# Modulation rows handed out along the mixer, and weight splits taken off GpSimd, in a hybrid DeltaNet layer

## The chip, the cores and the metric

The kernel runs on one core of a Trainium2 chip. The metric is the device time of one execution in microseconds (us). A core has TensorE (PE: matmuls, with weight loads shown as PEld), VectorE (DVE), ScalarE (ACT), GpSimd (POOL) and SyncE (SP), whose queue issues the transfers between memory and the on-chip buffers. Each engine takes its own instructions in the order in which they stand in its queue; semaphores hold one engine for another.

## What is computed

One decoder layer over 2048 tokens of width 1024. The vector c gives, through the weights w_ada, six rows of 1024 modulation values: shift, scale and gate for the mixer and for the feed-forward part.

```python
mod = (c_act @ w_ada[l] + b_ada[l])[:, None, :]
sh_m, sc_m, g_m, sh_f, sc_f, g_f = jnp.split(mod, 6, axis=-1)
h = rmsnorm(x, pre_mix_norm_w[l]) * (1.0 + sc_m) + sh_m
y = token_mixer(h, ...)
x = x + g_m * rmsnorm(y, post_mix_norm_w[l])
h = rmsnorm(x, pre_ffn_norm_w[l]) * (1.0 + sc_f) + sh_f
y = jnp.square(jax.nn.relu(h @ w_ff1[l])) @ w_ff2[l]
x = x + g_f * rmsnorm(y, post_ffn_norm_w[l])
```

The mixer projects h with w_in. One part is a gated delta rule with four heads (q, k, v through a short convolution, a recurrence over chunks whose state is carried from chunk to chunk, and an output gate z); the other is a gated short convolution of four groups (three projections each). Both go through w_out.

## The kernel before

The 2048 tokens are worked on in four blocks of 512, one behind the other; the change touches block 0, and three instructions at the start of block 1. A block is: norm and transpose of x, the mixer, the product with w_out (mix_out, L821), and the feed-forward part. Activations lie with the channels on the partitions. All projections are done with operands split in two parts (a rounded high part and the rest, "lo"), in three products: one tile of 128 output columns takes 8 x 3 = 24 matmuls of 128x512 (L336). The weights of a tile come as 512 KB from memory into a staging buffer (name w1s, 3 of them), are rounded by ScalarE (L250) and subtracted from (L251) by VectorE, or by GpSimd where the call says so, into a tile of the name w1h (3 of them). The first block keeps copies in memory for the later blocks (L288).

What the mixer does, by lines:

- L571 to L611: for two pairs of heads, twelve projections, each with a convolution (conv_silu, L430: ScalarE L436, VectorE three times L438, ScalarE L440), transposes (to_tm, L574) and sums of squares; pair_tail (L536) then forms for each pair the matrices Um and At, 16 of each of 128x128. Its last VectorE operation is L568.
- L622 to L649: the diagonal 32x32 blocks of Um go out to memory and come back side by side (L624, L630); VectorE inverts them by a substitution of 30 steps (L638, L640); the result goes out and comes back in place (L642 to L648).
- L657: block_inverse(t) builds block diagonals on GpSimd (L665) and does the rest of the inverse with short TensorE passes (L670 first). L695: scan(t) is one step of the recurrence over 128 tokens; its first products (L704) need only the state. block_inverse(t + 1) is written ahead of scan(t).
- L756 to L784: four projections for z, each evicted by one Silu on ScalarE (L762) into tiles of the name sb, then norm and gate of the recurrence's output. L786 to L812: the four short-conv groups, three projections each.
- L813: the gate and the second modulation are finished with column sums (L172, L192).

The modulation: w_ada has six parts of 1024 columns. Parts 0 and 1 are done at the start, part 5 in the feed-forward part. Here parts 2 (the mixer's gate, into the tile gate_m), 4 and 3 (scale and shift of the feed-forward part, into gate_f and a tile sb) are formed, each with eight rows of 128x1024, 24 in all. A row is one 512 KB load into a tile of the name w2h (3 of them, L129) and one VectorE operation on 128x1024 (L131 or L133). They were written as three jobs ahead of the first three short-conv groups (L618, L788).

What sets the order of the instructions: the program is written as quoted, and a scheduler lays each engine's queue out ahead of time, by data and buffers and in the order of the program where these leave a choice. So the place of an instruction in its queue is not the place of its line in the program. The projections for z and for the short-conv groups need nothing but h and weights, and the scheduler has put many of them ahead of the inverse. A tile of a name is given out in program order, and the next user of a buffer waits for the last reader of it. The accumulators of the projections (name acc) are four. Numbers behind a name (acc_1936) are running numbers of the tile in one kernel; they differ between the kernels.

Of the kernel before, what the change touches and what calls it, by code (L numbers as in the profile page):

```python
# [8 lines left out]
F32 = mybir.dt.float32  # L9
# [4 lines left out]
ALU = mybir.AluOpType  # L14

P = 128
# [4 lines left out]
TB = 512  # L21
# [11 lines left out]
def hybrid_layer(  # L33
# [90 lines left out]

    def ada_acc(part, acc):

        for k in range(KT):
            st = stage_w2h()
            nc.sync.dma_start(out=st, in_=w_ada[k * P:(k + 1) * P, part * DM:(part + 1) * DM])  # L129
            if k == 0:  # L130
                V.tensor_scalar(out=acc, in0=st, scalar1=c_act[:, 0:1], scalar2=None, op0=ALU.mult)  # L131
            else:
                V.scalar_tensor_tensor(out=acc, in0=st, scalar=c_act[:, k:k + 1], in1=acc,  # L133
                                       op0=ALU.mult, op1=ALU.add)
        return [acc[:, 0:TB], acc[:, TB:DM]]
# [294 lines left out]
    def conv_silu(ps, ft, dst):  # L430
# [6 lines left out]
        for w in range(3):  # L437
            V.scalar_tensor_tensor(out=tmp, in0=cb[:, w:w + TB], scalar=conv_w[:, w, ft:ft + 1],  # L438
                                   in1=tmp, op0=ALU.mult, op1=ALU.add)
        A.activation(out=dst, in_=tmp, func=AF.Silu)  # L440
# [82 lines left out]
    def mixer(b, hT, gates):  # L523
# [9 lines left out]
        rd = dram.tile([2, 4, 16, 32, 32], F32, name="rd")  # L533

        tails = []
        def pair_tail(pr, ssq, vfm):  # L536
# [12 lines left out]
            for hh in range(2):  # L549
# [7 lines left out]
                for tp0 in range(0, NT, 2):  # L557
# [4 lines left out]
                    for t in (tp0, tp0 + 1):  # L562
# [4 lines left out]
                                               op1=ALU.mult)  # L567
                        V.tensor_tensor(out=At[m // 8][:, m % 8, :], in0=pk[:, t - tp0, P:2 * P],  # L568
                                        in1=dt, op=ALU.mult)

        for pr in range(2):  # L571
# [17 lines left out]
            for hh in range(2):  # L589
                h = 2 * pr + hh  # L590
                for n, base in ((0, 4), (1, 0), (2, 8)):
                    if (pr, hh, n) == (0, 1, 1):
                        beta, eg, neg, dts = gates()
                    if early:
                        ps = early.pop(0)
                    else:
                        w = load_w1(w_in, (base + h) * P, (G, V, G)[n])
                        ps = ps_acc()
                        proj(ps, w, hT)
                    if n == 2:  # L600
                        vf = t2()
                        vfm.append(vf)
                    conv_silu(ps, base + h, vf if n == 2 else kq[h][:, n, :])
                    if tails and (hh, n) == (0, 1):
                        pair_tail(*tails.pop())
# [6 lines left out]

        if b == 0:
            gate_m = const.tile([P, DM], F32, name="gate_m")
            gate_f = const.tile([P, DM], F32, name="gate_f")
            ada["gate_m"], ada["gate_f"] = gate_m, gate_f
            acc_f = []
            jobs = [lambda: ada_acc(2, gate_m), lambda: acc_f.append(ada_acc(4, gate_f)),  # L618
                    lambda: acc_f.append(ada_acc(3, slot_b()))]

# [74 lines left out]
        def scan(t):  # L695
# [31 lines left out]
            for h0, m, um in pairs(t):  # L727
# [9 lines left out]
                for j in range(2):  # L737
                    h = h0 + j
                    V.scalar_tensor_tensor(out=S[h], in0=S[h], scalar=eg[:, 2, m + j:m + j + 1],
                                           in1=pg[:, j, P:2 * P], op0=ALU.mult, op1=ALU.add)  # L740
                V.tensor_tensor(out=om, in0=om, in1=pg[:, :, 0:P], op=ALU.add)

        wst = []
        block_inverse(0)
        for t in range(NT):
            if t + 1 < NT:
                block_inverse(t + 1)
            if t == NT - 1:
                for k in korder:
                    st = slot_a()  # L750
                    nc.sync.dma_start(out=st, in_=w_out[k * P:(k + 1) * P, :])
                    wst.append(st)
            scan(t)


        zs = [slot_b() for _ in range(2)]  # L756
        zh = [zs[h // 2][:, (h % 2) * TB:(h % 2 + 1) * TB] for h in range(NH)]
        for h in range(NH):
            w = load_w1(w_in, OFF_Z + h * P, (G, G, V, V)[h])
            ps = ps_acc()  # L760
            proj(ps, w, hT)
            A.activation(out=zh[h], in_=ps, func=AF.Silu)  # L762
# [23 lines left out]
        for f in range(4):  # L786
            if b == 0 and jobs:
                jobs.pop(0)()  # L788
            w = load_w1(w_in, OFF_SC + f * P)
# [23 lines left out]
        if b == 0:  # L813
            ada_gate(gate_m, 2, post_mix_norm_w)
            ada["f"] = [ada_affine(acc_f[0][i], acc_f[1][i], 100 + 4 * i, 68 + 4 * i, 92 + 4 * i, f"f{i}")
                        for i in range(2)]
# [348 lines left out]
```

## Time and profile before

| what | value |
| --- | --- |
| median of 3 runs | 2497.76 us (2494.24 to 2498.12) |
| the profiled execution | 2501.52 us, span 2499.8 us |
| TensorE busy | 2416.5 us (97%), 11874 matmuls |
| VectorE busy | 1764.7 us (71%) |
| ScalarE busy | 1170.9 us (47%) |
| GpSimd busy | 237.0 us (9%) |

The profiled execution is one run under the hardware profiler; its times are those of the rows below. A row of stretches gives the window, its length, and then for PE, PEld, DVE, ACT and POOL the busy time and in brackets the number of instructions, the granted TensorE clock as a share of full speed, the share of the transfer engines' time in use, and GB/s. A row by line gives line, engine, operation, out<-in and their shapes, count, busy time, mean duration, and behind the second bar how long the engine was idle just before these instructions and what ended that. Matmuls overlap, so the duration of one (0.39 us) is longer than the distance from one to the next.

### The profile page before, as it was taken

Reading aid. Unit: us, or ns where it says so; the run is one execution under the profiler, and the core shown is the slowest. Engines: PE = TensorE matmul, PEld = TensorE weight load, DVE = VectorE, ACT = ScalarE, POOL = GpSimd, SP = SyncE. Lnnn points to the kernel's source line nnn. Section 1 sums busy time; section 2 is a strip of 40 time slices with the busy share of each in tenths; the row PEclk is TensorE's granted clock in tenths of the full one; section 3 lists DMA queues with packets and bytes.
Section 4 is the critical chain, followed back from the end, with each engine's and each line's share of the span. In section 5 each row is a group of like instructions: output and inputs, shape, how many; then the busy total and the mean of one; then the engine's idle time right before and its main releaser. Section 6 shows DMA issues by size and latency. Waiting matters only on the chain.

```text
span 2499.8 us, 33806 instructions
## 1 busy us (share of the span) xinstructions
PE 2416.5 (97%) x11874; PEld 2011.4 (80%) x11874; DVE 1764.7 (71%) x3833; ACT 1170.9 (47%) x2402; POOL 237.0 (9%) x391
## 2 busy tenths in 40 slices
PE   5889999999999999999999999999999999999998
PEld 3678887788778888888878888888887888888887
DVE  6777795877885568576697657756679556857675
ACT  5533552444563245544466145544456424654432
POOL 2513010000040201000012020000002120100000
PEclk9999999999999999999999999999999999999999
DMA  7788489855664542544475544345557454344453
GB/s 246 266 292 267 168 292 310 283 177 169 202 234 156 172 153 103 156 147 127 136 245 193 184 154 143 102 135 152 160 164 249 143 169 168 110 144 135 125 161 101
DMA packets 297268, 449.53 MB, mean 180 GB/s; under 512 B 39189, under 2 KB 195978, under 8 KB 282250
## 3 DMA queue, kind: packets, MB, share of 16 engines
q1 hardware_dynamic: 295584, 447.27, 54.5%
q8 instruction: 94, 1.54, 0.3%
q14 instruction: 76, 0.62, 0.1%
q10 hardware_dynamic: 1514, 0.09, 0.0%
HBM read 376.01 MB, written 71.30 MB: 179 GB/s over the span
## 4 chain that ended last, share of the span: by engine, by line
PE 75%; DVE 13%; DMA 7%; ACT 3%; issue 2%; POOL 0%; SPq 0%; ACTq 0%; DVEq 0%
PE acc L336 41%; PE acc L341 24%; DVE t L438 2%; DMA w2h<-in_w_ff_dram 2%; DMA w2h<-in_w_ada_dram 1%; PE pd L704 1%; DMA w1s<-in_w_ff_dram 1%; PE pd L336 1%; DMA ws<-w2h 1%; DVE w1h L251 1%; DVE sb L935 1%; PE pd L560 1%; PE tp L265 1%; PE tp L692 1%; DVE sb L850 1%
## 5 line engine op out<-in xcount | busy, mean ns | idle before, releaser
L336 PE MATMUL acc<-h,w1h 128*128 128x512 f32 x5184 | 1219.6, 392 | 0.0
L336 PEld LDWEIGHTS acc<-h,w1h 128*128 128x128 f32 x5184 | 968.2, 188 | 196.0 <-ACT w1h L250 0.2
L341 PE MATMUL acc<-w1h,sa 128*128 128x512 f32 x2556 | 594.6, 392 | 7.9 <-ACT w1h L250 4.1
L341 PEld LDWEIGHTS acc<-w1h,sa 128*128 128x128 f32 x2556 | 478.3, 188 | 110.0 <-DVE w1h L251 7.0
L251 DVE TENSOR_TENSOR w1h<-w1s,w1h 128x1024 fp32r<-128x1024 f32 x333 | 406.5, 1221 | 152.8 <-ACT w1h L250 152.6
L250 ACT CAST w1h<-w1s 128x1024 fp32r<-128x1024 f32 (+1 forms) x343 | 359.6, 1048 | 289.2 <-PE acc L341 195.9
L959 DVE TENSOR_TENSOR t<-t 128x512 f32<-128x512 f32 (+1 forms) x148 | 91.3, 620 | 182.0 <-ACT t L958 179.2
L958 ACT ACTIVATE t<-acc 128x512 f32<-128x512 f32 (+1 forms) x132 | 73.7, 558 | 246.7 <-PE acc L336 246.3
L276 POOL TENSOR_TENSOR h<-t,h 128x256 fp32r<-128x256 f32 x70 | 59.6, 857 | 1251.9 <-ACT h L275 1246.6
L438 DVE SCALAR_TENSOR_TENSOR t<-cb,cols,t 128x512 f32<-128x512 f32 x144 | 119.1, 831 | 65.7 <-ACT t L436 63.9
L251 DVE TENSOR_TENSOR w2h<-sa,w2h 128x512 fp32r<-128x512 f32 x128 | 87.5, 687 | 35.7 <-ACT w2h L250 35.1
L336 PE MATMUL acc<-h,sa 128*128 128x256 f32 (+1 forms) x672 | 102.6, 308 | 4.0 <-POOL h L276 1.5
L250 ACT CAST w2h<-sa 128x512 fp32r<-128x512 f32 x128 | 78.5, 619 | 58.7 <-DVE w2h L251 33.2
L341 PE MATMUL acc<-w2h,sa 128*128 128x512 f32 x420 | 101.4, 393 | 0.0
L336 PEld LDWEIGHTS acc<-h,sa 128*128 128x128 f32 x672 | 90.2, 195 | 10.5 <-POOL h L276 3.8
L925 DVE TENSOR_TENSOR sb<-acc,sb 128x512 f32<-128x512 f32 x148 | 96.4, 681 | 2.0 <-PE acc L341 2.0
L341 PE MATMUL acc<-w2h,sb 128*128 128x512 f32 x384 | 95.2, 400 | 1.8 <-DVE sb L842 0.9
L341 PEld LDWEIGHTS acc<-w2h,sa 128*128 128x128 f32 x420 | 77.7, 188 | 15.5
L341 PEld LDWEIGHTS acc<-w2h,sb 128*128 128x128 f32 x384 | 72.3, 191 | 20.6 <-DVE sb L842 2.8
L250 ACT CAST sa<-t 128x256 fp32r<-128x256 f32 (+1 forms) x145 | 70.5, 487 | 27.2 <-DVE t L959 26.9
L251 DVE TENSOR_TENSOR sa<-t,sa 128x256 fp32r<-128x256 f32 (+2 forms) x145 | 75.3, 520 | 4.0 <-ACT sa L250 1.4
L234 ACT ACTIVATE jk_w<-sb 128x512 bf16<-128x512 f32 x64 | 40.3, 630 | 58.9 <-DVE sb L876 31.1
(285 smaller groups left out, 2748.4 us busy)
## 6 DMA issues: line engine op xcount, KB each, us to landing
w1s<-in_w_ff_dram SPq DMA_DIRECT2D x213, 512.0 KB, 3.9
w1h<-wc SPq DMA_DIRECT2D x86, 1024.0 KB, 4.9
w1s<-ws SPq DMA_DIRECT2D x112, 512.0 KB, 4.0
wc<-w1h SPq DMA_DIRECT2D x30, 1024.0 KB, 7.3
sa<-in_x_dram SPq DMA_DIRECT2D x32, 512.0 KB, 4.8
w1s<-in_w_in_dram SPq DMA_DIRECT2D x32, 512.0 KB, 5.4
w2h<-in_w_ada_dram SPq DMA_DIRECT2D x32, 512.0 KB, 5.3
sa<-in_w_out_dram SPq DMA_DIRECT2D x32, 512.0 KB, 3.8
```

Of the source, the lines that this page charges most:

```text
L234: A.activation(out=junk(DM, "w")[:, :src.shape[-1]], in_=src, func=AF.Square, scale=float(DM) ** -0.5, accum_out=s)
L250: A.copy(out=hi, in_=src)
L251: eng.tensor_tensor(out=lo, in0=src, in1=hi, op=ALU.subtract)
L265: T.transpose(out=tp[:, j * 256 + i * P:j * 256 + (i + 1) * P], in_=xn[i][:, (k0 + j) * P:(k0 + j + 1) * P], identity=ident)
L276: (G if j or eng is A else V).tensor_tensor(out=hT[k][:, 1, cs], in0=tmp, in1=hT[k][:, 0, cs], op=ALU.subtract)
L336: T.matmul(out=ps[:, c0:c1], lhsT=w[a][:, k, :], rhs=hT[k][:, b, c0:c1], start=(k == 0 and n == 0), stop=(k == KT - 1 and n == 2))
L341: T.matmul(out=ps, lhsT=lhs[a], rhs=rhs[b], start=(start and n == 0), stop=(stop and n == 2))
L438: V.scalar_tensor_tensor(out=tmp, in0=cb[:, w:w + TB], scalar=conv_w[:, w, ft:ft + 1], in1=tmp, op0=ALU.mult, op1=ALU.add)
L560: T.matmul(out=pk[:, t - tp0], lhsT=kq[h][:, 0, t * P:(t + 1) * P], rhs=kq[h][:, :, t * P:(t + 1) * P], start=True, stop=True)
L925: V.tensor_tensor(out=accs[key], in0=ps, in1=accs[key], op=ALU.add)
L958: A.activation(out=a[:, c0:c1], in_=ps[:, c0:c1], func=AF.Relu)
L959: V.tensor_tensor(out=a[:, c0:c1], in0=a[:, c0:c1], in1=a[:, c0:c1], op=ALU.mult)
```

## The change

Two things are changed.

The 24 modulation rows are no longer three jobs. ada_acc takes the rows that it does, and mod_rows(n) does the next n of the 24: one behind each of the twelve convolutions, three behind the last pair_tail, three each behind the scan steps 0, 1 and 2. tc.issue_after ties these operations, in the order of VectorE's queue, behind a named VectorE operation (the mark: the last L438 of a convolution, L568, or L741 of a scan step). The tile that takes part 3 (slot_b) is thereby taken behind scan step 0, ahead of the two tiles of z.

The weight splits that GpSimd did (ten: seven in block 0, three at the start of block 1) go to VectorE.

```diff
-    def ada_acc(part, acc):
+    def ada_acc(part, acc, ks=range(KT)):
-        for k in range(KT):
+        for k in ks:
...
         for w in range(3):
-            V.scalar_tensor_tensor(out=tmp, in0=cb[:, w:w + TB], scalar=conv_w[:, w, ft:ft + 1],
+            ada["mark"] = V.scalar_tensor_tensor(out=tmp, in0=cb[:, w:w + TB],
...
+        def mod_rows(n):
+            if b:
+                return
+            with tc.issue_after(ada["mark"].ins):
+                for _ in range(n):
+                    part, k = rows_left.pop(0)
+                    if part == 2:
+                        ada_acc(2, gate_m, [k])
+                    else:
+                        if k == 0:
+                            acc_f.append(gate_f if part == 4 else slot_b())
+                        ada_acc(part, acc_f[-1], [k])
...
-                        V.tensor_tensor(out=At[m // 8][:, m % 8, :], in0=pk[:, t - tp0, P:2 * P],
-                                        in1=dt, op=ALU.mult)
+                        ada["mark"] = V.tensor_tensor(out=At[m // 8][:, m % 8, :],
+                                                      in0=pk[:, t - tp0, P:2 * P], in1=dt,
+                                                      op=ALU.mult)
...
-                        w = load_w1(w_in, (base + h) * P, (G, V, G)[n])
+                        w = load_w1(w_in, (base + h) * P)
...
                     conv_silu(ps, base + h, vf if n == 2 else kq[h][:, n, :])
+                    mod_rows(1)
...
         pair_tail(*tails.pop())
-            jobs = [lambda: ada_acc(2, gate_m), lambda: acc_f.append(ada_acc(4, gate_f)),
-                    lambda: acc_f.append(ada_acc(3, slot_b()))]
+        mod_rows(3)
...
-                V.tensor_tensor(out=om, in0=om, in1=pg[:, :, 0:P], op=ALU.add)
+                ada["mark"] = V.tensor_tensor(out=om, in0=om, in1=pg[:, :, 0:P], op=ALU.add)
...
             scan(t)
+            if t < NT - 1:
+                mod_rows(3)
...
-            w = load_w1(w_in, OFF_Z + h * P, (G, G, V, V)[h])
+            w = load_w1(w_in, OFF_Z + h * P)
...
-            if b == 0 and jobs:
-                jobs.pop(0)()
```

The lines of the changed kernel have other numbers: L704 of before is L722, L670 is L688, L762 is L782, L674 is L692 and L766 is L786.

TensorE's queue in block 0, before, at the scan's first state products and where the inverse begins. Between the two stand 283 matmuls L336, for two accumulators of z (1863 and 1896) and ten of the short-conv groups (2054 to 2430):

```order
L704 MATMUL pd_1464<-S0_185,sa_598 128x128 x2
L704 MATMUL pd_1464<-S1_187,sa_599 128x128 x2
L336 MATMUL acc_1830<-h7_208,w1h_1826 128x512
L704 MATMUL pd_1474<-S2_189,sa_600 128x128 x2
L704 MATMUL pd_1474<-S3_191,sa_601 128x128 x2
L336 MATMUL acc_1863<-h0_201,w1h_1859 128x512 x3
...
L336 MATMUL acc_2430<-h5_206,w1h_2426 128x512 x3
L336 MATMUL acc_2430<-h6_207,w1h_2426 128x512
L670 MATMUL tp_1370<-sa_606,bd1_1367 128x128
L671 MATMUL tp_1370<-bd1_1367,sa_606 128x128
```

Behind this, the last five matmuls of that accumulator follow between the steps of the inverse.

The same place in the changed kernel. Between the two stand 36 matmuls L336, and they belong to two accumulators of z (1936 and 1969):

```order
L722 MATMUL pd_1509<-S0_185,sa_598 128x128 x2
L722 MATMUL pd_1509<-S1_187,sa_599 128x128 x2
L336 MATMUL acc_1936<-h3_204,w1h_1932 128x512
L722 MATMUL pd_1519<-S2_189,sa_600 128x128 x2
L722 MATMUL pd_1519<-S3_191,sa_601 128x128 x2
L336 MATMUL acc_1936<-h4_205,w1h_1932 128x512 x3
...
L336 MATMUL acc_1969<-h6_207,w1h_1965 128x512 x3
L336 MATMUL acc_1969<-h7_208,w1h_1965 128x512 x3
L688 MATMUL tp_1415<-sa_606,bd1_1412 128x128
L689 MATMUL tp_1415<-bd1_1412,sa_606 128x128
```

All twelve accumulators of the short-conv groups moved behind the first L688, two into the scan and ten after it.

ScalarE's queue in block 0, before, at the four evictions of z (L762); L250 rounds weights, L793 is a short-conv eviction:

```order
L440 ACTIVATE t2_1181<-t2_1186 128x512
L762 ACTIVATE sb_1788<-acc_1797 128x512
L250 CAST w1h_1892<-w1s_1889 128x1024
L762 ACTIVATE sb_1788<-acc_1830 128x512
L250 CAST w1h_2050<-w1s_2047 128x1024
L762 ACTIVATE sb_1789<-acc_1863 128x512
L250 CAST w1h_2084<-w1s_2081 128x1024
L762 ACTIVATE sb_1789<-acc_1896 128x512
L250 CAST w1h_2123<-w1s_2120 128x1024
L793 COPY scs_2079<-acc_2054 128x512
```

The same four evictions in the changed kernel (L782). L692 and L704 evict products of the inverse, here of block_inverse(2), and L786 squares the output of scan step 0:

```order
L692 COPY wt_1582<-tp_1577 128x512
L786 ACTIVATE jk_w_1996,sso_1995<-sa_1407,rqs_612 128x128
L692 COPY wt_1595<-tp_1590 128x512
L786 ACTIVATE jk_w_1998,sso_1995<-sa_1407,rqs_612 128x128
L786 ACTIVATE jk_w_2000,sso_1995<-sa_1407,rqs_612 128x128
L782 ACTIVATE sb_1861<-acc_1870 128x512
L782 ACTIVATE sb_1861<-acc_1903 128x512
L782 ACTIVATE sb_1862<-acc_1936 128x512
L704 COPY w2t_1603<-tp_1597 128x256
L782 ACTIVATE sb_1862<-acc_1969 128x512
```

The evictions of z moved from the end of the convolutions to a place behind the first scan step.

## Rows read from the trace of the kernel before

**Rows 1.** Stretches: window, length, busy us (instructions) per engine, clock, DMA.

```profile
123.20:161.00 37.80, 28.25 (x138) 23.44 (x138) 33.89 (x88) 16.88 (x50) 8.95 (x9) 0.91 0.81 282
161.00:225.30 64.30, 64.30 (x287) 53.24 (x286) 49.64 (x99) 15.71 (x22) 10.06 (x22) 1.00 0.81 252
225.30:266.80 41.50, 40.94 (x330) 38.88 (x329) 27.32 (x67) 25.36 (x77) 12.74 (x24) 1.00 0.85 303
```

**Rows 2.** TensorE's waits (total us, times, longest), 0 to 400 and 690 to 760.

```profile
PE tp L578 <- DVE bco L544: 9.2, 1, 9.2
...
PE tp L578 <- ACT sa L440: 2.8, 1, 2.8
```

**Rows 3.** Stretches around the longest wait of the mixer.

```profile
131.00:133.00 2.00, 0.57 (x3) 0.60 (x4) 1.97 (x10) 0.00 (x0) 0.20 (x1) 0.50 0.71 134
...
135.00:136.00 1.00, 1.00 (x5) 0.86 (x4) 0.69 (x1) 1.00 (x2) 0.00 (x0) 0.85 1.00 422
```

**Rows 4.** Single lines, block 0: ns min/median/max, first and last start us.

```profile
L568 DVE TENSOR_TENSOR sa<-pd,sa x16: 276/277/282, 133.2 to 158.9; 128x128 f32<-128x128 f32 x16
...
L633 DVE TENSOR_SCALAR sa<-sa x1: 677/677/677, 169.5 to 169.5; 64x1024 f32<-64x1024 f32 x1
...
L670 PE MATMUL tp<-sa,bd x32: 270/275/275, 225.3 to 249.3; 128*128 128x128 f32 x32
...
L172 PE MATMUL tp<-ones,sb x16: 250/250/250, 285.8 to 288.4; 128*128 128x1 f32 x16
```

**Rows 5.** TensorE by line (count | busy us, mean ns), 161 to 225.3.

```profile
L336 PE MATMUL acc<-h,w1h 128*128 128x512 f32 x283 | 64.4, 389 | 0.0
```

**Rows 6.** Groups by line, VectorE, 169.4 to 205.5.

```profile
L638 DVE TENSOR_TENSOR sa<-sa 64x30 f32<-64x30 f32 (+14 forms) x30 | 9.6, 321 | 0.9
L640 DVE TENSOR_TENSOR sa<-sa 64x30 f32<-64x30 f32 (+14 forms) x30 | 9.6, 320 | 0.7
L251 DVE TENSOR_TENSOR w1h<-w1s,w1h 128x1024 fp32r<-128x1024 f32 x7 | 8.5, 1214 | 8.0 <-ACT w1h L250 8.0
L804 DVE SCALAR_TENSOR_TENSOR scs<-cb,cols,scs 128x512 f32<-128x512 f32 x4 | 2.9, 737 | 0.0
```

**Rows 7.** Timeline (start us, duration us), 205 to 226, block 0.

```profile
205.42 1.13 DVE L643 COPY sa<-sa 64x1024 f32<-64x1024 f32 x1
...
210.00 4.82 SPq L648 DMA_DIRECT2D sa<-rd  x8
...
218.99 3.39 POOL L665 TENSOR_TENSOR bd<-sa,bdm 128x128 f32<-128x128 f32 x8
```

**Rows 8.** Timeline, 831 to 849, block 1.

```profile
831.67 1.13 DVE L643 COPY sa<-sa 64x1024 f32<-64x1024 f32 x1
...
840.97 3.37 POOL L665 TENSOR_TENSOR bd<-sa,bdm 128x128 f32<-128x128 f32 x8
```

**Rows 9.** Groups by line, GpSimd, whole span.

```profile
L251 POOL TENSOR_TENSOR w1h<-w1s,w1h 128x1024 fp32r<-128x1024 f32 x10 | 29.9, 2994 | 11.6 <-ACT w1h L250 11.6
```

**Rows 10.** Groups by line and shape, VectorE, 72 to 159.1.

```profile
L438 DVE SCALAR_TENSOR_TENSOR t<-cb,cols,t 128x512 f32<-128x512 f32 x36 | 34.5, 962 | 2.7 <-ACT t L436 2.5
L133 DVE SCALAR_TENSOR_TENSOR gate_m<-w2h,c_act,gate_m 128x1024 f32<-128x1024 f32 x7 | 11.1, 1584 | 4.5 <-DMA w2h<-in_w_ada_dram 4.5
L133 DVE SCALAR_TENSOR_TENSOR gate_f<-w2h,c_act,gate_f 128x1024 f32<-128x1024 f32 x7 | 8.9, 1278 | 0.3 <-DMA w2h<-in_w_ada_dram 0.3
```

**Rows 11.** Groups by line, TensorE, 266.7 to 288.6.

```profile
L341 PE MATMUL acc<-w2h,sb 128*128 128x512 f32 x29 | 9.2, 430 | 0.0
L336 PE MATMUL acc<-h,w1h 128*128 128x512 f32 x30 | 7.1, 393 | 0.0
```

**Rows 12.** Groups by line, TensorE, 225.3 to 266.8.

```profile
L336 PE MATMUL acc<-h,w1h 128*128 128x512 f32 x26 | 8.1, 419 | 0.0
```

**Rows 13.** Timeline, SyncE's queue, 240 to 300.

```profile
245.71 16.74 SPq L751 DMA_DIRECT2D sa<-in_w_out_dram  x8
```

**Rows 14.** Groups by line, TensorE, 288.5 to 500.

```profile
L341 PE MATMUL acc<-w1h,sa 128*128 128x512 f32 x268 | 64.5, 399 | 7.9 <-ACT w1h L250 4.1 <-DVE w1h L251 3.8
```

More of the change, by code (lines that the diff above doesn't have):

```diff
@@ L437, in conv_silu @@
         for w in range(3):
-            V.scalar_tensor_tensor(out=tmp, in0=cb[:, w:w + TB], scalar=conv_w[:, w, ft:ft + 1],
-                                   in1=tmp, op0=ALU.mult, op1=ALU.add)
+            ada["mark"] = V.scalar_tensor_tensor(out=tmp, in0=cb[:, w:w + TB],
+                                                 scalar=conv_w[:, w, ft:ft + 1], in1=tmp,
+                                                 op0=ALU.mult, op1=ALU.add)
         A.activation(out=dst, in_=tmp, func=AF.Silu)
@@ L533, in mixer @@
         rd = dram.tile([2, 4, 16, 32, 32], F32, name="rd")
+        if b == 0:
+            gate_m = const.tile([P, DM], F32, name="gate_m")
+            gate_f = const.tile([P, DM], F32, name="gate_f")
+            ada["gate_m"], ada["gate_f"] = gate_m, gate_f
+            acc_f = []
+            rows_left = [(part, k) for part in (2, 4, 3) for k in range(KT)]
+        def mod_rows(n):
[10 more added lines that the diff above has]
+                        ada_acc(part, acc_f[-1], [k])
         tails = []
@@ L611, in mixer @@
         pair_tail(*tails.pop())
[L613 to L617, printed above, removed]
-            jobs = [lambda: ada_acc(2, gate_m), lambda: acc_f.append(ada_acc(4, gate_f)),
-                    lambda: acc_f.append(ada_acc(3, slot_b()))]
+        mod_rows(3)
         for s in range(2):
@@ L814, in mixer @@
             ada_gate(gate_m, 2, post_mix_norm_w)
-            ada["f"] = [ada_affine(acc_f[0][i], acc_f[1][i], 100 + 4 * i, 68 + 4 * i, 92 + 4 * i, f"f{i}")
+            ada["f"] = [ada_affine(acc_f[0][:, i * TB:(i + 1) * TB],
+                                    acc_f[1][:, i * TB:(i + 1) * TB], 100 + 4 * i, 68 + 4 * i, 92 + 4 * i, f"f{i}")
                         for i in range(2)]
```

## The prediction

> **What bounds the kernel now.** I read the table by stretches first, to see which engine is full in block 0's mixer, then the list of what TensorE waited for, then the chain of VectorE, SyncE and GpSimd work that runs from the decay matrices to the scan. In the stretches, TensorE has work for nearly all of 161.0 to 266.8 us, and is short of it in the one ahead: from 123.2 on it is 28.3 us busy of 37.8 and VectorE 33.9, and it waits 9.2 us at one place, L578, for VectorE [rows 1, 2]. The granted clock, 1.00 in the stretches behind, is 0.50 in 131 to 133, when TensorE starts again (0.57 us of work there, so at 132.4), and on its way back, 0.85, in 135 to 136 [rows 3]. So up to 161 VectorE sets the pace, and from 161 on TensorE does.
>
> The stretch 161.0 to 225.3 is the one to understand. The 16 matrices Um are complete at 159.2 (start 158.9 plus 0.28), the first matmul of the blockwise inverse, L670, starts at 225.3 [rows 4]. In between the diagonal blocks go out to memory and back (L624, L630), VectorE runs the substitution L633 to L643, the result goes out and back again (L642 to L648), and GpSimd builds L665. This takes 66 us and costs TensorE nothing, because 283 projection matmuls of 0.2272 us (64.3 / 283) stand in its queue there [rows 5]. They are the cover. Everything below turns on whether the cover is still there.
>
> **The chain without its company.** VectorE starts L633 at 169.5, 10.3 us after Um [rows 4]. From there to the end of L643, at 206.6, are 37.1 us, but much of it is work of the short-conv groups put in between: seven weight splits of 1.21 us, four L804 and more. The chain's own part is L638 and L640 with the gaps ahead of them, 9.6 + 0.9 + 9.6 + 0.7 = 20.8, and L633 and L643, 0.7 and 1.1: 22.6 us [rows 4, 6, 7]. Behind L643 the eight loads L648 are issued up to 214.8 and L665 begins at 219.0; half of its eight operations (1.7 us) must be there for L670: 14.1 us after L643 [rows 7]. In block 1 the same way is 841.0 + 1.7 - 832.8 = 9.9 us [rows 8]. Together 10.3 + 22.6 + 1.2 (the one split that stays in it) + 9.9 to 14.1 = 44 to 48 us; I take 46.
>
> **What the change does to the cover.** The order of TensorE, shown with the change, has only 36 projection matmuls left between the scan's first state products and the inverse, instead of 283. The other 247 stand in the scan or behind it. The order of ScalarE says why: the four Silu evictions of z, which stood before the inverse, now stand in its third step (block_inverse(2)), so z holds all four accumulators until then, and no further projection can start. They stand there because the tile for the last modulation part is now taken, by program order, before the two tiles of z, and its first operation is tied behind the first scan step. Nothing in the program that needs this data is late; the matmuls are only in another place, and TensorE's queue is served in order, so it will stand at the inverse until the chain is done.
>
> **When TensorE gets there.** Up to the last Um VectorE sheds and gains. The splits on GpSimd go: 10 in all, 3.0 us each [rows 9], and while they ran VectorE's operations were stretched: 36 L438 had a mean of 0.962 where the same form takes 0.737 (L804), 36 x 0.225 = 8.1 us; the L133 of the gate had 1.584 against 1.278, 7 x 0.306 = 2.1 [rows 6, 10]. That is 10.2 us off. On it come, by VectorE's order up to the last Um, 13 weight splits where 5 stood (8 x 1.21 = 9.7), and 12 modulation rows instead of 15 (3 x 1.28 = 3.8 off). Net 10.2 + 3.8 - 9.7 = 4.3 us. The rows' loads are spread, so the 4.5 us in which VectorE waited for such a row [rows 10] may go as well: 159.2 - 4.3 - 4.5 = 150.4. Some waits for ScalarE, which gets the same casts closer together, will come instead: I take 152, with 159 (nothing gained) and 145 (twice the gain) as ends. Of the 43 matmuls behind the last products that Um needs (43 x 0.227 = 9.8 us) and the scan's eight state products (1 us) in its queue none waits for anything new: TensorE reaches the inverse at about 161, and the inverse can start at 152 + 46 = 198. **TensorE waits about 37 us** (30 to 43: an earlier Um moves both ends alike, a shorter or longer chain moves one).
>
> **The sum.** Before, TensorE needed 288.5 - 225.3 = 63.2 us from the first L670 to the last column sum of the mixer, L172, and 29 matmuls of mix_out (6.6 us) had already slipped in, so to the mixer's end alone 281.9 is the time to compare with [rows 4, 11]. By the order, 53 projection matmuls stand in those 63.2 us (the rows count 30 + 26, with those that an edge cuts [rows 11, 12]); now it is all 288 of the short-conv groups. The same stretch after: 63.2 - 6.6 + (288 - 53) x 0.2272 = 110.0. From 198 that ends at 308.0, and the clock after a wait costs 1.5 us (from 132.4 to about 135.4, 3 us at 0.50 did 1.5 us of work [rows 3]): 309.5 against 281.9, 27.6 us later. The three splits of block 1 that leave GpSimd can take about 1 us from a 2.8 us wait before L578 there [rows 2], or nothing. That leaves 26 to 27. From the feed-forward part of block 0 on, the orders are the same instruction by instruction, and TensorE is nearly full there (a rival below takes up the rest), so 26.5 us stay. The profiled execution took 2501.5 us (2499.8 of it the span) and would take 2528; the median of the runs shown is 2497.8, and 26.5 more are **2524 us**.
>
> A second count: TensorE's work is the same, only its waits differ. New is 37 and 1.5 for the clock; by the 152 above, 7 us sooner and 16 matmuls (3.6 us) further in its queue, 10.6 us of the old waits are gone. That is 27.9, less 1: the same within half a microsecond.
>
> **What else the change moves.** The modulation rows themselves (one operation of 1.28 us and one 512 KB load each) were spread over the mixer before as well: 15 of 24 stood before the last Um, 12 do now. The nine in the scan come behind operations that end a scan step, where VectorE is 27.3 us busy of 41.5 [rows 1]; 11.5 us fit, or cost up to 4 where a step waits on one. On SyncE's queue the row loads and four small loads for the gate now stand ahead of the inverse's loads, and the w_out loads ahead of six of the later short-conv weights. The latter were issued over 16.7 us, up to 262.5, close to the scan's end [rows 13]; four weight tiles (4 x 24 x 0.227 = 22 us of TensorE) are ready by then, so I cost it at nothing, and at 8 us if the tiles come one by one.
>
> **Rivals.**
> *The chain is quick (not slower).* With fewer transfers beside them, the two round trips through memory could shrink. The change costs nothing if Um to inverse takes 19 us instead of 46, or Um is ready at 125: then 2497. Against it: the substitution alone is 22.6 us, and no row gives VectorE 34 us to shed ahead of Um. Chance 0.04.
> *Part of it is given back.* In block 0's feed-forward stretch TensorE still waits 7.9 us for weight splits [rows 14], whose loads could run ahead while it stands, and the round trips may save some 4 us: 12 us less, 2512. For it: loads of weights do go ahead of their use; against it: only three tiles are free. Chance 0.12.
> *Weights late after the scan.* The 8 us above: 2532. Chance 0.04.
> *The clock stays low.* The wait is four times that of 9.2 us, after which the lower of the two levels (1.2 of 2.4 GHz) was granted for 3 us of work. If the scan's short passes, which follow at once, do not raise it, its 304 passes (330 - 26) of 0.117 us ((41.5 - 5.9) / 304) take twice as long: 35.6 more, 2558. Against it: the scan of before, with as many passes, has 1.00 throughout [rows 1]. Chance 0.06. Beside it stands the Trainium skill, "TensorE: Matmul & The Clock Gate", section "HAM oscillation — how this bites in real kernels": a wait for data that is too long makes the engine start cold, and a kernel pays this again at each such wait. The 0.50 of this trace agrees for one wait; by that rule alone only the restart is paid, which is the forecast, and the rival holds only if more waits inside the scan follow.
>
> **How the numbers follow.** The forecast has 0.74; its own range is 2513 to 2534, from the ends of the chain and of the old waits that go (Um at 145 or 159, chain 44 to 48). The range for 8 in 10 takes in the part given back and the late weights and leaves the clock and the quick chain out: 2510 to 2540. About 0.2% is what a measurement of this kernel can tell from no change, 5 us; faster than that 0.03, within it 0.03, slower 0.94.
>
> **What would show it.** In the profile after: TensorE idle for 30 to 43 us before the first matmul of the inverse, released by GpSimd's block diagonals; 36 projection matmuls ahead of it; no splits on GpSimd, and L438 at 0.74; the scan's start near 198, its end near 247; the short-conv projections in one solid stretch behind it; the granted clock at 0.50 for some us at the start of the inverse. I am wrong if TensorE is not idle there, if the chain is much shorter than 44 us, or if the last Um moves by more than 14 us.

## The result, and the profile after

The changed kernel takes 2519.8 us (median of 4 runs, 2518.8 to 2520.4) against 2497.9 for the kernel before (2494.2 to 2498.8): a ratio of 1.0083, 95% interval 1.0070 to 1.0096, so it is slower by 21.9 us. 2524 was forecast, with a range of 2510 to 2540. The profiled execution took 2519.8 us, span 2518.1; the one of before took 2501.5, above its own median, so the two traces differ by only 18.3 us, and the account below is in trace time.

What TensorE waited for in the changed kernel, from 60 to 420 us (total us, times, longest), is the answer to the first row of [rows 2]:

```profile
PE tp L688 <- POOL bd L683: 33.0, 1, 33.0
...
PE tp L601 <- DVE bco L566: 0.5, 1, 0.5
```

One wait of 33.0 us stands where none stood, ahead of the first pass of the inverse (L688, which is L670 of before). The old one of 9.2 us, ahead of L601 (L578 of before), is down to 0.5. Single lines of block 0 and the chain between them as a timeline answer to [rows 4] and [rows 7]:

```profile
L590 DVE TENSOR_TENSOR sa<-pd,sa x16: 278/282/283, 127.5 to 149.1; 128x128 f32<-128x128 f32 x16
...
L651 DVE TENSOR_SCALAR sa<-sa x1: 686/686/686, 159.9 to 159.9; 64x1024 f32<-64x1024 f32 x1
...
L688 PE MATMUL tp<-sa,bd x32: 275/275/582, 192.4 to 216.6; 128*128 128x128 f32 x32
...
L172 PE MATMUL tp<-ones,sb x16: 250/250/250, 301.2 to 305.6; 128*128 128x1 f32 x16
```

```profile
183.05 1.02 DVE L661 COPY sa<-sa 64x1024 f32<-64x1024 f32 x1
...
185.95 4.10 SPq L666 DMA_DIRECT2D sa<-rd  x8
...
189.75 1.68 POOL L683 TENSOR_TENSOR bd<-sa,bdm 128x128 f32<-128x128 f32 x4 [36.05 <-DMA sa<-rd]
```

The last Um is complete at 149.4 instead of 159.2 (by the end of L590, which forms the last At right behind it); VectorE starts the substitution (L651) at 159.9 and ends it (L661) at 184.1; the eight loads (L666) are issued by 190.1, GpSimd's block diagonals (L683) begin at 189.8, and TensorE gets going at 192.4: 43.0 us of chain, where 66 had been. TensorE has work for the first 10 us of it and then nothing, as its cover by line shows, 149.4 to 159.2, the answer to [rows 5]:

```profile
L336 PE MATMUL acc<-h,w1h 128*128 128x512 f32 x37 | 8.9, 394 | 0.0
L722 PE MATMUL pd<-S,sa 128*128 128x128 f32 x15 | 2.0, 274 | 0.0
```

(37 with the one between the state products L722.)

By the stretches the engine is nearly full on both sides of the wait, and restarts at the lower of its two clock levels:

```profile
123.20:161.00 37.80, 35.69 (x176) 28.85 (x174) 31.76 (x85) 14.47 (x44) 5.01 (x12) 1.00 0.90 301
161.00:200.00 39.00, 7.30 (x39) 6.92 (x40) 22.34 (x64) 4.11 (x9) 6.71 (x16) 0.56 0.58 191
200.00:250.00 50.00, 50.00 (x353) 45.69 (x352) 38.58 (x87) 28.55 (x84) 9.80 (x19) 1.00 0.61 204
250.00:310.00 60.00, 59.95 (x284) 48.65 (x283) 35.07 (x62) 19.18 (x38) 1.12 (x6) 1.00 0.77 269
...
192.00:194.00 2.00, 1.58 (x7) 1.58 (x8) 0.00 (x0) 0.00 (x0) 1.61 (x4) 0.50 0.00 0
194.00:196.00 2.00, 2.00 (x12) 2.00 (x10) 0.00 (x0) 0.59 (x1) 0.87 (x2) 0.50 0.04 8
196.00:198.00 2.00, 2.00 (x13) 2.00 (x13) 0.13 (x1) 0.59 (x1) 0.87 (x2) 0.63 0.00 0
198.00:200.00 2.00, 1.72 (x13) 1.34 (x13) 1.14 (x3) 0.75 (x2) 1.60 (x4) 1.00 0.00 0
```

0.50 from 192.4 on and 0.63 in 196 to 198 is about 5 us at the lower level, so some 2.5 us lost (an estimate from these rows). From there to the mixer's end nothing more is late: the 288 projection matmuls of the short-conv groups, all of them now behind the first pass of the inverse, run nearly without a gap (59.95 busy of 60 from 250 to 310), and the last L172 ends at 305.9, 8 matmuls of mix_out (1.8 us) having slipped in: 304.0 to compare with 281.9, 22.1 us later. The first matmul of mix_out on the recurrence's heads comes 20.2 us later than before (314.9 against 294.7), block 1's first inverse pass 19.0, the end 18.3.

VectorE's answer to the first of [rows 10], by line and shape, 72 to 159.1, shows what was gained ahead of the wait:

```profile
L438 DVE SCALAR_TENSOR_TENSOR t<-cb,cols,t 128x512 f32<-128x512 f32 x36 | 28.6, 801 | 0.1
```

Without GpSimd's splits beside it the operation has a mean of 0.80 us instead of 0.96.

### The profile page after: what moved, and what is told of

The parts are those of the page before. It is cut to its first block, busy times and chain, and to the rows that moved or that the text cites. A ratio compares the mean times of both kernels' runs of the same rounds, so it can differ in the third digit from the quotient of the medians.

```text
span 2518.1 us, 33786 instructions
## 1 busy us (share of the span) xinstructions
PE 2418.2 (96%) x11874; PEld 2013.3 (80%) x11874; DVE 1768.1 (70%) x3843; ACT 1174.9 (47%) x2404; POOL 206.2 (8%) x381
## 4 chain that ended last, share of the span: by engine, by line
PE 77%; DVE 12%; DMA 5%; ACT 3%; issue 2%; SPq 0%; POOL 0%; ACTq 0%; DVEq 0%; POOLq 0%
PE acc L336 42%; PE acc L341 26%; DVE t L438 2%; PE pd L722 1%; DMA ws<-w2h 1%; PE pd L336 1%; DMA w2h<-in_w_ff_dram 1%; DVE w1h L251 1%; DVE sa L510 1%; PE pd L582 1%; PE tp L265 1%; DMA w1s<-in_w_ff_dram 1%; DVE sb L869 1%; PE tp L710 1%; PE tp L698 1%
## 5 line engine op out<-in xcount | busy, mean ns | idle before, releaser
L336 PE MATMUL acc<-h,w1h 128*128 128x512 f32 x5184 | 1224.0, 393 | 4.4 <-DMA w1h<-wc 4.4
L336 PEld LDWEIGHTS acc<-h,w1h 128*128 128x128 f32 x5184 | 967.9, 188 | 201.1 <-DMA w1h<-wc 5.2
L341 PE MATMUL acc<-w1h,sa 128*128 128x512 f32 x2556 | 595.3, 392 | 5.4 <-ACT w1h L250 3.7
L341 PEld LDWEIGHTS acc<-w1h,sa 128*128 128x128 f32 x2556 | 479.0, 188 | 107.5 <-DVE w1h L251 4.3
L251 DVE TENSOR_TENSOR w1h<-w1s,w1h 128x1024 fp32r<-128x1024 f32 (+1 forms) x343 | 420.0, 1225 | 157.6 <-ACT w1h L250 157.1
L250 ACT CAST w1h<-w1s 128x1024 fp32r<-128x1024 f32 (+1 forms) x343 | 359.5, 1049 | 315.2 <-PE acc L341 199.1
L438 DVE SCALAR_TENSOR_TENSOR t<-cb,cols,t 128x512 f32<-128x512 f32 x144 | 115.1, 803 | 65.4 <-ACT t L436 63.7
L336 PE MATMUL acc<-h,sa 128*128 128x256 f32 (+1 forms) x672 | 103.1, 309 | 3.1 <-ACT h L275 1.5
L250 ACT CAST w2h<-sa 128x512 fp32r<-128x512 f32 x128 | 78.6, 620 | 56.9 <-DVE w2h L251 37.1
L341 PE MATMUL acc<-w2h,sa 128*128 128x512 f32 x420 | 101.4, 393 | 0.0
L336 PEld LDWEIGHTS acc<-h,sa 128*128 128x128 f32 x672 | 90.9, 196 | 9.2 <-POOL h L276 2.8
L341 PE MATMUL acc<-w2h,sb 128*128 128x512 f32 x384 | 91.4, 393 | 1.5 <-DVE sb L861 0.8
L341 PEld LDWEIGHTS acc<-w2h,sa 128*128 128x128 f32 x420 | 77.7, 188 | 15.5
L341 PEld LDWEIGHTS acc<-w2h,sb 128*128 128x128 f32 x384 | 71.2, 188 | 19.7 <-DVE w2h L251 2.8
L250 ACT CAST sa<-t 128x256 fp32r<-128x256 f32 (+1 forms) x145 | 70.3, 485 | 26.2 <-DVE t L978 25.7
```

Of the source, the lines that this page charges most:

```text
L250: A.copy(out=hi, in_=src)
L251: eng.tensor_tensor(out=lo, in0=src, in1=hi, op=ALU.subtract)
L336: T.matmul(out=ps[:, c0:c1], lhsT=w[a][:, k, :], rhs=hT[k][:, b, c0:c1], start=(k == 0 and n == 0), stop=(k == KT - 1 and n == 2))
L341: T.matmul(out=ps, lhsT=lhs[a], rhs=rhs[b], start=(start and n == 0), stop=(stop and n == 2))
L438: ada["mark"] = V.scalar_tensor_tensor(out=tmp, in0=cb[:, w:w + TB], scalar=conv_w[:, w, ft:ft + 1], in1=tmp, op0=ALU.mult, op1=ALU.add)
```

## The experiments

The theory: the time is lost because the projections that covered the inverse's chain were put behind it, and they were put there because one tile of a shared pool (part 3's, name sb) is first used behind scan step 0, ahead of z's tiles from the same pool. The rivals: the ties to the scan steps cost by themselves; the splits on VectorE carry the loss; something else of the chain is late. In each kernel the number of projection matmuls between the scan's first state products and the first inverse pass was read from TensorE's order; it is the "cover".

| kernel | cover | TensorE's wait at the inverse | median us | ratio to before, 95% interval |
| --- | --- | --- | --- | --- |
| before | 283 | none | 2498 | 1 |
| changed | 36 | 33.0 | 2519.8 | 1.0083 (1.0070 to 1.0096) |
| parts 3 and 4 swapped | 276 | none | 2488.4 | 0.9962 (0.9947 to 0.9977) |
| part 3 in its own tile | 276 | none | 2486.3 | 0.9946 (0.9932 to 0.9959) |
| z written early | 168 | 4.5 | 2502.0 | 1.0015 (1.0004 to 1.0027) |
| rows ahead | 300 | 3.8 | 2498.6 | 1.0002 (0.9991 to 1.0013) |
| splits alone | 276 | none | 2492.9 | 0.9970 (0.9956 to 0.9983) |
| rows handed out alone | 52 | 32.1 | 2527.8 | 1.0117 (1.0096 to 1.0139) |
| part 3 alone | 59 | 30.1 | 2541.2 | 1.0167 (1.0152 to 1.0182) |
| swapped, block 1 as before | 276 | none | 2485.9 | 0.9952 (0.9939 to 0.9965) |
| own tile, block 1 as before | 276 | none | 2487.9 | 0.9957 (0.9943 to 0.9971) |
| splits alone, block 0 only | 276 | none | 2489.9 | 0.9964 (0.9952 to 0.9976) |

### The cover put back: the parts swapped, and an own tile

```diff
-            rows_left = [(part, k) for part in (2, 4, 3) for k in range(KT)]
+            rows_left = [(part, k) for part in (2, 3, 4) for k in range(KT)]
...
+            acc_f.reverse()
```

> The changed kernel, but parts 3 and 4 of the modulation are formed in the other order, so that the shared tile for part 3 is first used in the second pair of heads and not behind scan step 0. VectorE's queue is the same up to the last Um; 276 projection matmuls stand ahead of the inverse instead of 36. Theory (the loss is the missing cover): the last Um stays at 149, the chain takes 43 us plus some 14 of short-conv work put back into it, the inverse can start near 207, the cover lasts to 212; TensorE's wait of 33 us at the first inverse pass is gone, the 10.6 us of old waits stay gone: 2482 to 2488. Rival (the rows tied to the scan steps, or VectorE's extra splits, cost the time): the wait may go, but the time stays near 2510 to 2520.

The second kernel leaves the parts in their order and changes the tile alone:

```diff
-                            acc_f.append(gate_f if part == 4 else slot_b())
+                            acc_f.append(gate_f if part == 4 else const.tile([P, DM], F32, name="acc3"))
```

> The changed kernel with one difference: part 3 of the modulation is formed in a tile of its own, not in one of the seven tiles sb that z and the short-conv groups share. All rows stay where the change put them, nine of them tied behind the scan steps. The order shows 276 projection matmuls ahead of the inverse. Theory (the shared tile, first used behind scan step 0, holds back z's tiles behind it, and so the cover): no wait at the inverse, 2485 to 2492, as with the parts swapped. Rival (the tie of nine rows to the scan steps is what costs): over 2505.

With the own tile the last Um and the first inverse pass are, by lines:

```profile
L590 DVE TENSOR_TENSOR sa<-pd,sa x16: 280/281/285, 127.5 to 149.3; 128x128 f32<-128x128 f32 x16
...
L688 PE MATMUL tp<-sa,bd x32: 270/275/348, 213.6 to 235.8; 128*128 128x128 f32 x32
```

With the own tile the last Um is where the changed kernel has it (started at 149.3, there 149.1; with the parts swapped it starts 2 us later, at 151.1), the inverse begins at 213.6, 64 us behind it, and no wait for the block diagonals is left in either kernel. 2486.3 us lies in the theory's span, 2488.4 is 0.4 above its own, both far from the rivals'. The own tile tells the two apart most clearly: its nine rows are tied behind the same scan steps as in the changed kernel, and it takes 33.5 us less. So the ties by themselves don't make the loss; the shared tile, first used behind one of them, does.

### Half of the cover put back: z written early

The four projections of z, with their weights and Silu (L775 to L782 of the changed kernel), are moved in the program from behind the scan to ahead of it, in all blocks.

```diff
+        zs = [slot_b() for _ in range(2)]
...
+            A.activation(out=zh[h], in_=ps, func=AF.Silu)
         wst = []
         block_inverse(0)
```

> The changed kernel with the four z projections written ahead of the scan instead of behind it. 168 projection matmuls stand between the first state products and the inverse, and 168 more than in the changed kernel stand ahead of the inverse in all. Theory (the wait is the chain less the cover, matmul for matmul): 168 matmuls are 38 us of cover, the chain grows by 8 us of short-conv work put back into it, and Um may come some us later behind the added matmuls, so the wait falls from 33 to 3 to 11 us, and the time from 2520 to 2490 to 2498. Rival (the wait doesn't go by the number of matmuls, since something else is late): a wait over 25 us.

What TensorE waited for, 60 to 420 and, below, from 420 to the end:

```profile
PE tp L688 <- POOL bd L683: 4.5, 1, 4.5
...
PE tp L688 <- POOL bd L683: 5.7, 5, 1.8
```

The wait fell to 4.5 us, within the 3 to 11 reckoned from the count of matmuls. The time missed its span by 4 us, at least in part because the edit also moves z in the other blocks, where TensorE now waits at the inverse five more times, 5.7 us in all. From the first inverse pass of block 1 to that of block 2 it takes 601.1 us, where the kernel before takes 596.6 and the changed one 596.9.

### Rows out of the scan, into the chain

```diff
-        mod_rows(3)
+        mod_rows(12)
...
-            if t < NT - 1:
-                mod_rows(3)
```

> The changed kernel with the nine rows taken out of the scan: all twelve remaining rows stand behind the last pair's matrices, ahead of the inverse; part 3 stays in the shared tile. The order shows 300 projection matmuls ahead of the inverse. Theory (the shared tile does harm only where its first use is tied to a scan step): 12 rows of 1.28 us between the last Um and the substitution make the chain start some 6 us later, so the inverse can start at 149 + 43 + 12 + 6 = 210, and 300 matmuls of cover last to 217: no wait, 2484 to 2492. Rival (rows must not stand in the chain): a wait of 5 us or more at the inverse, 2494 or more.

Part 3 stays in the shared tile here, and the cover is the largest of all. So the tile takes the cover away only where its first use is tied behind a scan step. But the chain got longer than expected: the wait at the inverse is not gone.

```profile
PE acc L336 <- ACT w1h L250: 5.0, 1, 5.0
PE tp L688 <- POOL bd L683: 3.8, 1, 3.8
...
L651 DVE TENSOR_SCALAR sa<-sa x1: 682/682/682, 177.1 to 177.1; 64x1024 f32<-64x1024 f32 x1
```

The timeline of SyncE's queue shows why the substitution starts at 177.1 and not at 166:

```profile
148.87 1.33 SPq L642 DMA_DIRECT2D ud<-sa  x3
151.18 3.24 SPq L129 DMA_DIRECT2D w2h<-in_w_ada_dram  x3
154.47 0.42 SPq L642 DMA_DIRECT2D ud<-sa  x1
158.14 8.77 SPq L129 DMA_DIRECT2D w2h<-in_w_ada_dram  x6
166.96 1.91 SPq L642 DMA_DIRECT2D ud<-sa  x4
...
172.42 0.52 SPq L648 DMA_DIRECT2D sa<-ud  x1
```

Six row loads (L129) stand in the queue ahead of the last four of the eight transfers that carry Um's diagonal blocks out (L642). Each of them waits until VectorE has used up one of three staging tiles, and the queue waits with it: 8.8 us for the six. The rows cost here through the queue, not through VectorE's 1.28 us each. The theory's time (2484 to 2492) is missed by 7; the rival's is met, though the wait that it names is 3.8 and not 5, and one of 5.0 for the rounding of weights stands beside it.

### Each half of the change alone

Only the splits, on the kernel before:

```diff
-                        w = load_w1(w_in, (base + h) * P, (G, V, G)[n])
+                        w = load_w1(w_in, (base + h) * P)
...
-            w = load_w1(w_in, OFF_Z + h * P, (G, G, V, V)[h])
+            w = load_w1(w_in, OFF_Z + h * P)
```

> The kernel before, with only the ten splits moved from GpSimd to VectorE; the modulation rows stay three jobs. 276 projection matmuls ahead of the inverse. Theory (GpSimd's splits held VectorE back ahead of the last Um): last Um at 150 to 155, the wait of 9.2 us shrinks to 0 to 5, no wait at the inverse: 2483 to 2492. Rival (the spreading of the rows is what freed VectorE): 2495 to 2500, and the 9.2 us wait stays.

And the changed kernel with these two lines as they were before, so only the rows are handed out:

> The changed kernel with the ten splits back on GpSimd, so only the rows are handed out. 52 projection matmuls ahead of the inverse. Theory: the whole loss sits in this part: last Um at 155 to 158, TensorE waits 26 to 32 us at the first inverse pass, part of the old 9.2 us wait stays: 2524 to 2532, slower than the changed kernel. Rival (the splits carry the loss): 2496 to 2500.

The last Um of the first, by line, its wait, and the wait of the second:

```profile
L568 DVE TENSOR_TENSOR sa<-pd,sa x16: 280/282/284, 123.0 to 150.9; 128x128 f32<-128x128 f32 x16
...
PE tp L578 <- DVE bco L544: 2.4, 1, 2.4
```

```profile
PE tp L688 <- POOL bd L683: 32.1, 1, 32.1
PE acc L336 <- POOL w1h L251: 3.1, 1, 3.1
PE tp L601 <- DVE bco L566: 3.0, 1, 3.0
```

With the splits alone the last Um is ready at 151.2, 8 us sooner, and the wait of 9.2 is 2.4: the mechanism is the theory's, the time 2492.9 just above its span, and not the rival's. With the rows handed out alone the last Um comes at 154.4, just ahead of the 155 to 158 expected, and the whole loss is there, 29 us by the ratio, and part of the old waits with it (3.1 for a split on GpSimd, 3.0 ahead of L601). So the hand-out loses and the splits gain, and the second is hidden in the sum.

The mean of L438, which reads two operands from the on-chip memory, falls from 0.96 us [rows 10] to 0.77 with the splits alone:

```profile
L438 DVE SCALAR_TENSOR_TENSOR t<-cb,cols,t 128x512 f32<-128x512 f32 x36 | 27.1, 770 | 0.0
```

The Trainium skill ("SBUF — State Buffer", section "Who interferes with whom") says that a VectorE instruction with two such inputs contends with a GpSimd instruction that reads the same memory, over a shared port pair. These two means agree with it.

### One part of the hand-out alone

The kernel before, with only the eight rows of part 3 tied behind scan steps 0 to 2; the other 16 rows stay jobs.

```diff
-                    lambda: acc_f.append(ada_acc(3, slot_b()))]
+        def part3(t):
+            with tc.issue_after(ada["mark"].ins):
+                if t == 0:
+                    acc_f.append(slot_b())
+                ada_acc(3, acc_f[0], range(3 * t, min(3 * t + 3, KT)))
...
             scan(t)
+            if t < NT - 1:
+                part3(t)
```

> The kernel before with one part of the change: the eight rows of part 3 are tied behind scan steps 0 to 2, in a tile sb; the other 16 rows stay two jobs and the splits stay on GpSimd. The order shows 59 projection matmuls ahead of the inverse, and none of the 16 rows ahead of the last Um (they use the same three staging tiles behind part 3's). Theory: this part alone makes the loss: the last Um at 145 to 152, since 15 rows are gone from ahead of it, chain 43 to 45, TensorE waits 26 to 34 us at the first inverse pass: 2512 to 2528. Rival (the loss needs the twelve rows behind the convolutions, or the splits on VectorE): 2490 to 2502, with no wait at the inverse.

What TensorE waited for, 60 to 420, VectorE's waits for ScalarE, 60 to 157, and the stretch behind the scan:

```profile
PE tp L677 <- POOL bd L672: 30.1, 1, 30.1
PE acc L336 <- DVE w1h L251: 4.6, 2, 4.2
...
PE acc L336 <- ACT w1h L250: 2.1, 1, 2.1
...
DVE t L438 <- ACT t L436: 12.0, 4, 4.8
...
253.20:300.00 46.80, 39.03 (x157) 29.48 (x156) 43.34 (x78) 14.82 (x25) 2.75 (x4) 0.90 0.89 302
```

The wait is as expected and nothing of the rest of the change is in it, so part 3 alone makes the wait. Two expectations failed. The last Um came at 156.0 and not at 145 to 152: with the 15 rows gone from ahead of it VectorE waited for ScalarE's part of the convolutions instead, 12.0 us (2.5 before, [rows 10]). And the time is 13 us above its span: all 24 rows now stand behind the start of the scan, and from 253 to 300 VectorE is 43.3 us busy of 46.8 while TensorE waits 6.7 us for weights to be rounded and split and has a clock of 0.90. That late pile I had not counted. What it costs of the 13 us is not shown.

### Block 1's three splits

With all ten splits moved a new wait shows up in block 1, of the same size in the changed kernel and in the one with swapped parts. With block 1's three back on GpSimd the old wait of [rows 2] returns instead:

```profile
PE acc L336 <- DMA w1h<-wc: 4.4, 1, 4.4
```

```profile
PE tp L601 <- ACT sa L441: 2.9, 1, 2.9
```

```diff
-                        w = load_w1(w_in, (base + h) * P)
+                        w = load_w1(w_in, (base + h) * P, V if b == 0 else (G, V, G)[n])
...
-            w = load_w1(w_in, OFF_Z + h * P)
+            w = load_w1(w_in, OFF_Z + h * P, V if b == 0 else (G, G, V, V)[h])
```

The same edit was made to the kernel with swapped parts, to the one with an own tile, and to the one with the splits alone.

> The changed kernel with parts 3 and 4 swapped, and the three splits of block 1 back on GpSimd, so only block 0's seven are moved. With all ten moved TensorE waits 4.4 us near 727 for prepared weights (L336, released by the load w1h<-wc) and the clock falls behind that; the kernel before has 2.8 us before L578 there instead. Theory (the 4.4 us wait comes with the three splits): it is gone, the 2.8 us is back, 1 to 4 us less than with the parts swapped alone: 2484 to 2488. Rival (it comes with the earlier arrival in block 1): the wait stays, 2488 to 2491.

> The changed kernel with part 3 in a tile of its own, and the three splits of block 1 left on GpSimd. Theory: no wait at the inverse (276 matmuls of cover), and in block 1 the 2.9 us wait for ScalarE in place of the 4.1 us wait for prepared weights: 2482 to 2487. Rival (the splits of block 1 are worth their move): 2487 to 2490, above the own tile with all ten moved.

> The kernel before with only the seven splits of block 0 moved to VectorE: neither rows handed out nor block 1 touched. Theory (the rows' place is worth little by itself, the seven splits carry the gain): within 3 us of the kernel with parts swapped and block 1's splits on GpSimd: 2485 to 2491. Rival (handing the rows out is worth something once the tile is not in the way): 4 us or more behind it.

The waits trade places as the theory says. The times bear out only the first of the three spans (2485.9). The second misses its theory's by 0.9 us and lies in the rival's (2487.9), and the third is inside the theory's span but 4.0 us behind the kernel that it is compared with, where the rival begins. So what block 1's splits are worth is not settled: 2485.9 against 2488.4 with the parts swapped speaks for GpSimd in block 1, 2487.9 against 2486.3 with the own tile against it, and the intervals overlap. Nor do the runs settle whether the rows handed out rightly are worth something over the splits alone: 2485.9 against 2489.9 (0.9952 and 0.9964, intervals overlapping) with block 1 untouched, 2486.3 against 2492.9 (0.9946 and 0.9970, just overlapping) with all ten moved.

Both kernels are beaten by each version that has the cover and no wait at the inverse. The lowest ratio is that of the own tile, 0.9946 (0.9932 to 0.9959), 33.5 us below the changed kernel.

## Why the prediction was right, step by step

**The cover.** Right: 36 matmuls and a wait of 33.0 us (37 were forecast, 30 to 43 as ends), in the place named and released by GpSimd's block diagonals.

**The chain.** 46 us were taken, 43.0 came. The three pieces: from Um to the substitution 10.5 (10.3 taken); the substitution with one split 24.2 (23.8); from its end to the first pass 8.3 (9.9 to 14.1). The last piece was mis-sized, below both rows that it was taken from; why the loads and GpSimd were quicker here was not tested.

**The last Um.** 152 taken, 149.4 measured, but not by the terms of the sum, so that it came so near is in part luck. Up to the last Um, before and after:

```profile
0.00:159.20 159.20, 115.11 (x517) 89.87 (x518) 117.60 (x237) 83.72 (x193) 59.38 (x58) 0.98 0.77 260
0.00:149.40 149.40, 117.23 (x530) 92.27 (x531) 115.93 (x242) 86.22 (x195) 42.68 (x51) 0.98 0.80 268
...
DVE w1h L251 <- ACT w1h L250: 2.3, 2, 1.4
```

VectorE's work fell by 1.7 us (117.6 to 115.9), where the sum had 4.3: L438 alone gave 5.9 us (34.5 to 28.6) instead of 8.1. Its idle time fell by 8.1 us (41.6 to 33.5), where the sum had 4.5 for a row less 1.6 for new waits on ScalarE. Those did come (the 2.3 us above), but old waits for TensorE (2.7 us less at L452, which is L451 of before) and for ScalarE (2.5 at L438) went with the one for the row.

**From the inverse to the mixer's end.** 110.0 and 1.5 for the clock were taken, 111.6 came (304.0 less 192.4). The clock itself was mis-sized: about 5 us at the lower level and not 3, so 2.5 us and not 1.5; the stretch without it took about 1 us less than reckoned.

**The sum.** Um (2.6) and the chain (3.0) make 5.6 us of the miss: 22.1 at the mixer's end instead of 27.6. Between there and mix_out 1.9 us more came off, which the sum had not, and behind that another 1.9 instead of 1, the balance of larger steps (given back, below). That gives 18.3 in the traces; between the medians it is 21.9, since the profiled execution of before was 3.6 us above its median. The forecast of 2524 was 4 us too high.

**What set the order.** The prediction put it down to part 3's tile being taken ahead of z's, with its first use tied behind scan step 0. The runs bear that out as far as they go: an own tile for part 3 gives the cover back with all ties in place, an earlier first use does (swapped), and tied behind the matrices Um instead of a scan step it leaves the cover where it was (rows ahead). A kernel in which z's two tiles are only requested earlier, with their first use where it was, gets the same order as the changed kernel (36 matmuls of cover), so what counts seems to be not where the tile is asked for but where it is first used. Only its order is known; it was not run.

**The rivals.** The quick chain fell: 43.0 us, not 19. Late weights after the scan: no wait there (the reason given counts four weight tiles, the kernel has three, name w1h; nothing hung on it). The low clock: it was back at 1.00 about 5 us after the restart, while the inverse's short passes ran. The rule of the Trainium skill ("TensorE: Matmul & The Clock Gate", section "HAM oscillation — how this bites in real kernels"), that a long wait for data is followed by a cold start, agrees with this trace: one wait of 33.0 us, one restart at 0.50, paid once.

*Part of it is given back* came in part, and the sentence that 26.5 us stay from the feed-forward part on did not hold step by step. 1.9 us came off in mix_out. In block 0's feed-forward part the waits for weights fell from 7.9 us [rows 14] to 5.1, and at the start of block 1 short old waits shrank from 4.1 us in all (660 to 700) to 1.3 (678 to 717). Between the first and the last of that part's second products (L341, before and after) the delay fell from 20.3 us to 15.4:

```profile
L341 PE MATMUL acc<-w1h,sa 128*128 128x512 f32 x277 | 67.2, 402 | 5.1 <-ACT w1h L250 3.7 <-DVE w1h L251 1.3
...
L341 PE MATMUL acc<-w1h,sa x696: 387/389/675, 384.4 to 699.6; 128*128 128x512 f32 x174
...
L341 PE MATMUL acc<-w1h,sa x696: 387/389/796, 404.7 to 715.0; 128*128 128x512 f32 x174
```

The new wait of 4.4 us in block 1 and the lower clock behind it then took most of that back, and block 1's inverse is 19.0 us late. That the end is nearly as late as mix_out (18.3 and 20.2) is luck: the sum had neither the gain nor the loss.

**What failed.** "L438 at 0.74": it is at 0.80, so GpSimd's splits were not all that stretched it. Two of the 36 took 1.78 and 1.77 us while GpSimd was at L519, an operation with a 128x512 operand that the change leaves there; the other 34 have a mean of 0.744:

```profile
96.63 8.63 POOL L519 TENSOR_TENSOR sa<-sa,tri 128x512 f32<-128x512 f32 x4
...
98.41 1.78 DVE L438 SCALAR_TENSOR_TENSOR t<-cb,cols,t 128x512 f32<-128x512 f32 x1
...
102.33 1.77 DVE L438 SCALAR_TENSOR_TENSOR t<-cb,cols,t 128x512 f32<-128x512 f32 x1
```

The kernel before has two such as well (1.79 and 1.77, beside L518 of its lines). So of the 8.1 us that the prediction put down to the splits, 5.9 were theirs.

## What to carry to other kernels

Before a piece of work is tied behind a later step, look at what it shares with the work that fills the wait of that step: a tile from a common pool, a staging buffer, a transfer queue. In a pool that is given out in order the tie is passed on to the users behind it, and here one tile of 4 KB a partition kept 247 matmuls from standing where they hid the chain (43 us by itself). The order of the engine that must not wait, read between the last thing that it gives and the first thing that it needs, shows such a loss as a count of instructions before anything is timed.

## What the runs showed that I had not expected

Transfers that wait for a buffer hold up the queue for others that are ready. With twelve rows behind the last Um, six loads that waited for three staging tiles took 8.8 us on SyncE's queue, and the last four of the eight transfers for the inverse, whose data was there at 150 us, went out at 167.0.

Moving block 1's three splits off GpSimd removed a 2.8 us wait and made one of 4.4 for a load of prepared weights, with the clock at 0.52 for the 5 us behind it:

```profile
732.00:737.00 5.00, 5.00 (x14) 3.84 (x14) 5.00 (x17) 1.26 (x2) 1.18 (x2) 0.52 0.26 106
737.00:742.00 5.00, 5.00 (x31) 4.29 (x30) 4.51 (x12) 4.31 (x15) 0.26 (x1) 1.00 0.71 299
```
